# Where the dot products of the second residual gate stand: in the merge or behind the second row block, in a two-layer encoder trunk on one Trainium2 core

## The chip, the cores and the metric

The kernel runs on one core of one Trainium2 chip. The core has five engines that run side by side, each with its own queue of instructions in a fixed order: TensorE (PE in the profile, with its weight loads as PEld), VectorE (DVE), ScalarE (ACT), GpSimd (POOL) and SyncE (SP), which here only issues the transfers of the weights from the chip's memory. An instruction starts when the one before it on its engine is done and the semaphores that it waits for have been raised. The metric is device microseconds (us) of one execution of the whole program, less is better.

## The reference

A bidirectional encoder of two layers on 256 positions of 1024 channels, all in float32. Each layer adds two sub-layers to the residual x, both steered by a vector c:

```python
c_act = silu(c)
for l in range(2):
    mod = c_act @ ada_w[l] + ada_b[l]            # 6 x 1024 numbers
    sh1, sc1, g1, sh2, sc2, g2 = split(mod, 6)
    h = rmsnorm(x, norm1_g[l]) * (1 + sc1) + sh1
    x = x + g1 * token_mix(h, w_in[l], w_fourier[l], w_ret[l], w_out[l])
    h = rmsnorm(x, norm2_g[l]) * (1 + sc2) + sh2
    x = x + g2 * conv_ffn(h, ffn_up[l], conv_w[l], conv_b[l], ffn_down[l])
return rmsnorm(x, final_g)
```

`token_mix` projects h, runs a Fourier branch and a retention branch, maps each to 1024 channels, and merges them: sigmoid(a_f) * y_f + sigmoid(a_r) * y_r, followed by an output projection. `conv_ffn` projects h up to two halves of 2816 channels, convolves each over three positions, multiplies gelu(first) by the second and projects down. The gate g2 is needed only after the down-projection, at the end of the layer.

## The kernel before, in words

**Precision and weights.** Each float32 operand is split into a high part of a shorter format and the rest; a product takes three matmuls (high x high, high x low, low x high: lines 149 to 151 with activations as the standing operand, line 157 with weights). So every weight block is prepared on the core: `raw()` (line 67) loads 1 MB (128 x 2048 floats) through SP into one of four raw buffers; then for each half `split` (line 61) makes the high part on ScalarE (line 63) and the low part on VectorE (line 64). A half takes one of four `wt` buffers, or a `wb` buffer of the pool for activations, where the table `plan` says so. `nextw` hands out the blocks in the order of `plan` and prepares one block ahead. A raw buffer is free again when its last reader is done, a `wt` buffer when TensorE has used it.

**Modulation vectors.** The 6 x 1024 numbers are not computed on TensorE: `ada_dots` (line 201) loads a quarter of one vector's weights (1 MB, into the same four raw buffers) and runs two dot products of 128 x 1024 with the broadcast c on VectorE (`ada_dot`, line 191; "ISA" in the order, CUSTOM_DVE_ANT_0 in the profile). Four quarters make a vector. `ada_col` does so for shift and scale (`c_sh`, `c_sc`, by way of `sct`), `ada_gate` for a gate: its dots land in `gc`, and after the fourth quarter `rows` transposes `gc` on TensorE (line 225), copies it (line 227) and sends it through memory to all partitions (lines 229 and 230). For the second gate `rows` is put into the list `behind` and is run later, in the up-projection.

**Where the quarters stand.** Lists of quarters are made per layer: G1 and G2 (gates), SC and SH (scale and shift of the second sub-layer), NX1 (the next layer's). `pl` sorts them into places, and `side(where, n)` runs the next n of a place there. In layer 0, place `h` (after each retention head) has G1, and place `c` (the merge) has SC, SH and G2 in turn, three to each of four columns. In layer 1, place `h` has SC, and place `c` has SH and G2 in turn, two to a column. Place `d` is the down-projection.

**The merge** (list MERGE, line 28; loop at line 621) goes through four columns of 256 channels, each in four steps: the two sigmoid projections, the Fourier map and the retention map. One step takes one weight block, 48 matmuls of 256 columns in two halves. At the end of a column VectorE multiplies and adds (lines 632 and 636), the result is split into `mg`, and `side("c", ...)` runs. Then the **output projection** takes four blocks wo0 to wo3 (`in_wx_dram`): wo0 and wo1 in `wt` buffers, wo2 and wo3 in `wb` buffers; for row block m = 0 and then m = 1 (128 positions each) it multiplies `mg` by all four, adds to the residual (lines 317 and 318), and prepares the normed and modulated h of the second sub-layer, `hT2` (`norm_mod`, `modulate`).

**The FFN's up-projection** does its first NX = 3 of 22 channel blocks by row blocks (loop at line 683, result `ut`): m = 0 while `hT2` of the second row block is still in the making, then m = 1. Their transposes and convolutions (`t_gated`) are put off with `later`, to be run between the halves of the blocks j = 3, 4, 5. From j = 3 on, a block is one weight block, 48 matmuls with both row blocks as one moving operand of 256 columns, then two convolutions on ScalarE (line 664) and VectorE (lines 665 and 668), a gelu, a product (line 677) and a split. `tick` counts half blocks and runs what `later` has put off.

**Order.** The program is traced in the order in which it is written; a scheduler then orders each engine's queue by readiness, with priority to what was traced first, and gives out the buffers. `tc.issue_after(ins)` forces what is traced under it behind `ins` on the engine of `ins`.

Of the kernel before, what the change touches and what calls it, by code (L numbers as in the profile page):

```python
# [21 lines left out]
NX = 3  # L22
# [6 lines left out]
def trunk(ctx, tc, a, out):  # L29
# [19 lines left out]
    def ps():  # L49
        return pp.tile([P, 512], F32, tag="ps", name="ps")  # L50
# [47 lines left out]
        plan += [(a["down"][l][:, t * 2048 : (t + 1) * 2048], int(t >= NT - 2), 0) for t in range(NT)]  # L98
    ready = []
    state = {"at": 0}  # L100
    hold = []

    def ahead(n):
# [26 lines left out]
    behind = []  # L130

    def later(n, fn):
        waiting.append([n, fn])

    def tick():
        for z in waiting:
            z[0] -= 1
        due = [z for z in waiting if z[0] <= 0]
        waiting[:] = [z for z in waiting if z[0] > 0]
        for _, fn in due:  # L140
            fn()
# [99 lines left out]
    def rstd(ss):  # L241
        V.tensor_scalar(out=ss[:, 0:1], in0=ss[:, 0:1], scalar1=ss[:, 1:2], scalar2=EPS, op0=ALU.add, op1=ALU.add)
        r = sp.tile([P, 1], F32, tag="rs", name="rs")
        G.tensor_tensor(out=r, in0=ss[:, 0:1], in1=nhalf[:, 0:1], op=ALU.pow)
        return r
# [13 lines left out]
    def norm_t(xn, pt=None):  # L259

        pt = pt or ps()
        for b in range(4):
            T.transpose(pt[:, b * P : (b + 1) * P], xn[:, b * P : (b + 1) * P], ident)  # L263
        return pt

    def modulate(l, i, m, hf, src, h, b0=0, nb=4):

        t = tmp("hm")
        for b in range(b0, b0 + nb):
            k = hf * 4 + b  # L270
            s = slice(b * P, (b + 1) * P)
            sc, sh = scA[l][i][:, k : k + 1], shB[l][i][:, k : k + 1]
            if (b + m) % 2 == 0 or nb == 1:
                A.activation(t[:, s], src[:, s], AF.Identity, scale=sc, bias=sh)  # L274
            else:
                V.tensor_scalar(out=t[:, s], in0=src[:, s], scalar1=sc, scalar2=sh, op0=ALU.mult, op1=ALU.add)
        z = slice(b0, b0 + nb)
        return split(h[:, 0, z, tok(m)], h[:, 1, z, tok(m)], t.rearrange("p (b t) -> p b t", b=4)[:, z, :])

    def norm_mod(l, i, m, hp, ss, t0, t1):  # L280

        def mod(hf):
            made = modulate(l, i, m, hf, norm_t(xns[hf]), hp[hf])
            if i == m == 0:
                hold[:] = [2, *made]

        r = rstd(ss)
        xns = [norm_s(m, r, hf) for hf in range(2)]
        for hf, t in ((0, t0), (1, t1)):
            later(t, lambda hf=hf: mod(hf))  # L290
# [12 lines left out]
    def mm_w(pt, hp, w, cut=None):  # L303


        for b in range(2):
            for k in range(KT):
                s = slice(k * P, (k + 1) * P)
                x, t = hp[k // 4], w[b]
                mm_ws(pt[:, b * S : (b + 1) * S], t[:, 0, s], t[:, 1, s], x[:, 0, k % 4, :], x[:, 1, k % 4, :],  # L310
                      k == 0, k == KT - 1, b == cut and k == 0)
            tick()
# [50 lines left out]
    for k in range(KT):  # L363
# [12 lines left out]
        for z in range(2):  # L376
            t = wt()[:, :2048].rearrange("p (s c) -> p s c", s=2)
            nh = 2 if k == 0 else 1
            for n in range(nh):
                c = slice(n * D // nh, (n + 1) * D // nh)  # L380
# [25 lines left out]
    for l in range(L):  # L406
# [50 lines left out]
        G1 = [lambda q=q: ada_gate(l, 0, q, gc1, g1) for q in range(4)]  # L457
        G2 = [lambda q=q: ada_gate(l, 1, q, gc2, g2) for q in range(4)]
        SC = [lambda q=q: ada_col(l, 1, 1, q) for q in range(4)]
        SH = [lambda q=q: ada_col(l, 1, 0, q) for q in range(4)]  # L460
        NX1 = [lambda q=q, kind=kind: ada_col(l + 1, 0, kind, q) for kind in (1, 0) for q in range(4)] if l + 1 < L else []
        if l == 0:
            pl = dict(v=[], h=G1, c=[z[i] for i in range(4) for z in (SC, SH, G2)], d=NX1)
        else:
            pl = dict(v=G1, h=SC, c=[SH[i // 2] if i % 2 == 0 else G2[i // 2] for i in range(8)], d=NX1)

        def side(where, n):
            for _ in range(n):
                if pl[where]:
                    pl[where].pop(0)()  # L470
# [212 lines left out]
        for m in range(2):  # L683
            if m == 1:
                flush()
            for j in range(NX):
                o = ps()[:, :S]
                for k in range(KT):
                    s = slice((k % 4) * S, (k % 4 + 1) * S)
                    x, t = hp2[k // 4], wx[j][k // 4]  # L690
                    mm_xs(o, x[:, 0, k % 4, tok(m)], x[:, 1, k % 4, tok(m)], t[:, 0, s], t[:, 1, s],
                          k == 0, k == KT - 1)
                if m == 1:
                    ahead((j + 1) // 2)
                ut[m][j] = tmp("ut")[:, :S]
                A.activation(ut[m][j], o, AF.Copy)
                tick()

        def t_gated(j):
# [5 lines left out]

        for j in range(NX):
            later(2 * j + 1, lambda j=j: t_gated(j))
        while behind:
            later(2 * NX - 1, behind.pop())
        for j in range(NX, FT):  # L710
            w = nextw()
            pt = ps()
            mm_w(pt, hp2, w, 1 if j == 2 * NX - 1 else None)
            gated(pt, j)

# [140 lines left out]
```

## Time and profile before

| | us |
|---|---|
| median of three runs | 889.98 (887.55 to 890.5) |
| profiled execution, whole | 888.77 |
| its span in the trace | 886.9 |
| TensorE busy | 867.5 |
| VectorE busy | 736.7 |
| ScalarE busy | 501.8 |

The span runs from the first to the last instruction that the profiler saw; the execution's own time has 1.9 us around it. In rows of the trace, the first number is the start in us from the span's start, the second the duration, then engine, line, operation and tiles as out<-in, with xcount where equal rows are merged; square brackets give the engine's idle time before the row and what ended it. In rows of waits, the three numbers are the total in us, the number of waits and the longest. In rows of stretches, each engine has its busy time and its instruction count, then come the granted clock of TensorE (1.00 is full), the busy share of the DMA engines and the GB/s that they moved. Names of the trace leave out buffer numbers; `hT2` appears there as `hT`.

Where the parts lie in the trace: the merge of layer 0 from about 150 to 237.7, its output projection to 263, the up-projection to about 387; in layer 1 the output projection begins at 670.8 and the up-projection's blocks j >= 3 at 713.1.

### The profile page before, as it was taken

Reading aid. Unit: us, or ns where it says so; the run is one execution under the profiler, and the core shown is the slowest. Engines: PE = TensorE matmul, PEld = TensorE weight load, DVE = VectorE, ACT = ScalarE, POOL = GpSimd, SP = SyncE. Lnnn points to the kernel's source line nnn. Section 1 sums busy time; section 2 is a strip of 40 time slices with the busy share of each in tenths; the row PEclk is TensorE's granted clock in tenths of the full one; section 3 lists DMA queues with packets and bytes.
Section 4 is the critical chain, followed back from the end, with each engine's and each line's share of the span. In section 5 each row is a group of like instructions: output and inputs, shape, how many; then the busy total and the mean of one; then the engine's idle time right before and its main releaser. Section 6 shows DMA issues by size and latency. Waiting matters only on the chain.

```text
span 886.9 us, 15356 instructions
## 1 busy us (share of the span) xinstructions
PE 867.5 (98%) x6250; PEld 809.2 (91%) x6250; DVE 736.7 (83%) x1135; ACT 501.8 (57%) x736; POOL 22.1 (2%) x33
## 2 busy tenths in 40 slices
PE   7999999999899999999999999999999999999996
PEld 5889999999889999998888899999998999999885
DVE  6899998888785899999787789878887769999554
ACT  5666445544465877653574554555444768777442
POOL 1000010000000000000000000000000000000000
PEclk9999999999999999999999999999999999999999
DMA  8995665788883465579856667637887455655521
GB/s 319 357 377 208 234 224 208 256 334 311 328 311 145 144 214 198 197 261 376 345 190 222 250 224 266 219 125 284 299 328 275 144 190 197 222 200 191 190 96 48
DMA packets 33032, 210.84 MB, mean 238 GB/s; under 512 B 4001, under 2 KB 4289, under 8 KB 10178
## 3 DMA queue, kind: packets, MB, share of 16 engines
q1 hardware_dynamic: 31682, 207.16, 63.7%
q0 software_dynamic: 704, 2.11, 0.7%
q8 instruction: 49, 0.80, 0.4%
q10 hardware_dynamic: 576, 0.59, 0.2%
q14 instruction: 21, 0.17, 0.1%
HBM read 208.79 MB, written 1.06 MB: 237 GB/s over the span
## 4 chain that ended last, share of the span: by engine, by line
PE 75%; DVE 13%; DMA 5%; ACT 3%; issue 3%; POOL 1%; POOLq 0%; SPq 0%; ACTq 0%; DVEq 0%
PE ps L157 41%; PE ps L150 11%; PE ps L149 11%; PE ps L151 11%; DVE wt L64 5%; DMA raw<-in_ada_dram 3%; DVE raw L193 3%; PE ps L263 1%; ACT wt L63 1%; DMA raw<-in_ww_dram 1%; DMA raw<-in_wx_dram 1%; PE ps L481 1%; DVE qk L64 1%; ACT hm L274 1%; DVE sig L632 0%
## 5 line engine op out<-in xcount | busy, mean ns | idle before, releaser
L157 PE MATMUL ps<-hT,wt 128*128 128x256 f32 (+1 forms) x3368 | 390.6, 277 | 0.0
L157 PEld LDWEIGHTS ps<-hT,wt 128*128 128x128 f32 x3368 | 386.6, 188 | 0.4
L63 ACT ACTIVATE wt<-raw 128x1024 fp32r<-128x1024 f32 (+1 forms) x270 | 281.9, 1052 | 181.2 <-PE ps L157 72.4
L64 DVE TENSOR_TENSOR wt<-raw,wt 128x1024 fp32r<-128x1024 f32 (+1 forms) x270 | 325.4, 1214 | 56.3 <-ACT wt L63 55.3
L193 DVE CUSTOM_DVE_ANT_0 raw<-raw,c_cbc,c_adab 128x1024 f32<-128x1024 f32 x96 | 121.2, 1279 | 17.8 <-DMA raw<-in_ada_dram 17.8
L151 PE MATMUL ps<-wt,hT 128*128 128x512 f32 (+1 forms) x240 | 87.1, 363 | 0.0
L150 PE MATMUL ps<-wt,hT 128*128 128x512 f32 (+1 forms) x240 | 87.0, 363 | 0.0
L149 PE MATMUL ps<-wt,hT 128*128 128x512 f32 (+1 forms) x240 | 83.8, 366 | 2.5 <-ACT wt L63 2.3
L664 ACT ACTIVATE cv<-ps,c_cvw 128x256 f32<-128x256 f32 x88 | 49.4, 562 | 29.2 <-PE ps L157 18.6
L150 PE MATMUL ps<-wt,act 128*128 128x512 f32 (+1 forms) x162 | 59.4, 367 | 0.0
L149 PE MATMUL ps<-wt,act 128*128 128x512 f32 (+1 forms) x162 | 59.3, 366 | 0.0
L151 PE MATMUL ps<-wt,act 128*128 128x512 f32 (+1 forms) x162 | 59.2, 365 | 0.0
L149 PEld LDWEIGHTS ps<-wt,hT 128*128 128x128 f32 x240 | 45.2, 189 | 10.6 <-ACT wt L63 3.2
L151 PEld LDWEIGHTS ps<-wt,hT 128*128 128x128 f32 x240 | 45.5, 190 | 7.4
L150 PEld LDWEIGHTS ps<-wt,hT 128*128 128x128 f32 x240 | 45.5, 190 | 6.8
L665 DVE SCALAR_TENSOR_TENSOR cv<-ps,c_cvw,cv 128x255 f32<-128x255 f32 x88 | 41.1, 479 | 6.4 <-ACT cv L664 6.4
L157 PE MATMUL ps<-yf,wt 128*128 128x256 f32 x384 | 45.0, 277 | 0.0
L157 PE MATMUL ps<-yrT,wt 128*128 128x256 f32 x384 | 45.0, 277 | 0.0
L157 PEld LDWEIGHTS ps<-yrT,wt 128*128 128x128 f32 x384 | 44.3, 188 | 0.0
L157 PEld LDWEIGHTS ps<-yf,wt 128*128 128x128 f32 x384 | 44.3, 188 | 0.0
L668 DVE SCALAR_TENSOR_TENSOR cv<-ps,c_cvw,cv 128x255 f32<-128x255 f32 x88 | 41.2, 480 | 1.6
L149 PEld LDWEIGHTS ps<-wt,act 128*128 128x128 f32 x162 | 30.6, 189 | 5.1
(154 smaller groups left out, 942.0 us busy)
## 6 DMA issues: line engine op xcount, KB each, us to landing
raw<-in_ww_dram SPq DMA_DIRECT2D x48, 1024.0 KB, 5.5
raw<-in_ada_dram SPq DMA_DIRECT2D x40, 1024.0 KB, 5.9
raw<-in_up_dram SPq DMA_DIRECT2D x38, 1024.0 KB, 4.8
raw<-in_wx_dram SPq DMA_DIRECT2D x24, 1024.0 KB, 6.6
raw<-in_down_dram SPq DMA_DIRECT2D x22, 1024.0 KB, 4.9
raw<-in_ada_dram SPq DMA_DIRECT2D x16, 512.0 KB, 8.4
raw<-in_wx_dram SPq DMA_DIRECT2D x16, 512.0 KB, 7.9
raw<-in_upx_dram SPq DMA_DIRECT2D x6, 1024.0 KB, 6.6
```

The source lines that it names most:

```text
L63: h = A.activation(dst_h, src if hi_src is None else hi_src, AF.Copy)
L64: l = V.tensor_tensor(out=dst_l, in0=src, in1=dst_h.bitcast(F32), op=ALU.subtract)
L149: T.matmul(pt, xh, wh, start=start, stop=False)
L150: T.matmul(pt, xh, wl, start=False, stop=False)
L151: T.matmul(pt, xl, wh, start=False, stop=stop)
L157: T.matmul(pt[:, z], w, x[:, z], start=start and i == 0, stop=stop and i == 2)
L193: V.tensor_tensor_reduce(out=wb, in0=wb, in1=cbc, scale=1.0, scalar=adab[:, l, v * KT + k : v * KT + k + 1], op0=ALU.mult, op1=ALU.add, ac ...
L263: T.transpose(pt[:, b * P : (b + 1) * P], xn[:, b * P : (b + 1) * P], ident)
L274: A.activation(t[:, s], src[:, s], AF.Identity, scale=sc, bias=sh)
L664: A.activation(o, pt, AF.Identity, scale=cvw[:, l, 1, c : c + 1], bias=cvw[:, l, 3, c : c + 1])
L665: V.scalar_tensor_tensor(out=o[:, 1:], in0=pt[:, : S - 1], scalar=cvw[:, l, 0, c : c + 1], in1=o[:, 1:], op0=ALU.mult, op1=ALU.add)
L668: V.scalar_tensor_tensor(out=o[:, : S - 1], in0=pt[:, 1:], scalar=cvw[:, l, 2, c : c + 1], in1=o[:, : S - 1], op0=ALU.mult, op1=ALU.add)
```

## The change

The four quarters of G2 leave the merge in both layers. They get a place of their own, `u`, in the up-projection: one quarter after each of the three channel blocks of the second row block, and the last one when block j = 3 begins. The dots of the first three are forced behind the last split of `hT2` on VectorE (`last_h[1]`, noted by `mod` in `norm_mod`). The rest of the gate (`rows`, by way of `behind`) is put off at block j = 3 and runs after as many half blocks as before. In the merge, layer 0 now has two quarters to a column, layer 1 one.

```diff
@@ -98,6 +98,7 @@
         plan += [(a["down"][l][:, t * 2048 : (t + 1) * 2048], int(t >= NT - 2), 0) for t in range(NT)]
     ready = []
     state = {"at": 0}
+    last_h = []
     hold = []
 
     def ahead(n):
@@ -283,6 +284,7 @@
             made = modulate(l, i, m, hf, norm_t(xns[hf]), hp[hf])
             if i == m == 0:
                 hold[:] = [2, *made]
+            last_h[:] = made
 
         r = rstd(ss)
         xns = [norm_s(m, r, hf) for hf in range(2)]
@@ -460,9 +462,9 @@
         SH = [lambda q=q: ada_col(l, 1, 0, q) for q in range(4)]
         NX1 = [lambda q=q, kind=kind: ada_col(l + 1, 0, kind, q) for kind in (1, 0) for q in range(4)] if l + 1 < L else []
         if l == 0:
-            pl = dict(v=[], h=G1, c=[z[i] for i in range(4) for z in (SC, SH, G2)], d=NX1)
+            pl = dict(v=[], h=G1, c=[z[i] for i in range(4) for z in (SC, SH)], u=G2, d=NX1)
         else:
-            pl = dict(v=G1, h=SC, c=[SH[i // 2] if i % 2 == 0 else G2[i // 2] for i in range(8)], d=NX1)
+            pl = dict(v=G1, h=SC, c=SH, u=G2, d=NX1)
 
         def side(where, n):
             for _ in range(n):
@@ -694,6 +696,9 @@
                     ahead((j + 1) // 2)
                 ut[m][j] = tmp("ut")[:, :S]
                 A.activation(ut[m][j], o, AF.Copy)
+                if m == 1:
+                    with tc.issue_after(last_h[1]):
+                        side("u", 1)
                 tick()
 
         def t_gated(j):
@@ -705,11 +710,12 @@
 
         for j in range(NX):
             later(2 * j + 1, lambda j=j: t_gated(j))
-        while behind:
-            later(2 * NX - 1, behind.pop())
         for j in range(NX, FT):
             w = nextw()
             pt = ps()
+            if j == NX:
+                side("u", 1)
+                later(2 * NX - 1, behind.pop())
             mm_w(pt, hp2, w, 1 if j == 2 * NX - 1 else None)
             gated(pt, j)
```

How this moves VectorE's queue at the end of layer 0's merge. The names: `raw_2625` and `raw_2630` hold the last quarters of scale and shift, `raw_2634` the last of G2; `wt_2566` and `wt_2569` are the halves of wo0 (`raw_2564`), `wt_2640` and `wt_2643` of wo1 (`raw_2638`); L632 and L636 are the merge's products and sum in `sig`. Before, from the product of the last column's third step on:

```order
L632 TENSOR_TENSOR sig_2444<-ps_2505,sig_2444 128x512
L64 TENSOR_TENSOR wt_2569<-raw_2564,wt_2569 128x1024
L193 ISA raw_2630,c_sh01_98<-raw_2630,c_cbc_73,c_adab_78 128x1024
L193 ISA c_sh01_98 128x1
L193 ISA raw_2634,gc_599<-raw_2634,c_cbc_73,c_adab_78 128x1024
L193 ISA gc_599 128x1
L193 ISA raw_2634,gc_599<-raw_2634,c_cbc_73,c_adab_78 128x1024
L193 ISA gc_599 128x1
L632 TENSOR_TENSOR sig_2503<-ps_2563,sig_2503 128x512
L64 TENSOR_TENSOR wt_2640<-raw_2638,wt_2640 128x1024
L636 TENSOR_TENSOR sig_2444<-sig_2444,sig_2503 128x512
L64 TENSOR_TENSOR wt_2643<-raw_2638,wt_2643 128x1024
```

In the change (the numbers of buffers and lines differ: `wt_2557` is the second half of wo0, `wt_2624` and `wt_2627` are wo1, `wb_2632` and `wb_2635` wo2):

```order
L634 TENSOR_TENSOR sig_2432<-ps_2493,sig_2432 128x512
L64 TENSOR_TENSOR wt_2557<-raw_2552,wt_2557 128x1024
L64 TENSOR_TENSOR wb_2632<-raw_2630,wb_2632 128x1024
L64 TENSOR_TENSOR wt_2624<-raw_2622,wt_2624 128x1024
L634 TENSOR_TENSOR sig_2491<-ps_2551,sig_2491 128x512
L64 TENSOR_TENSOR wb_2635<-raw_2630,wb_2635 128x1024
L638 TENSOR_TENSOR sig_2432<-sig_2432,sig_2491 128x512
L64 TENSOR_TENSOR wt_2627<-raw_2622,wt_2627 128x1024
L64 TENSOR_TENSOR mg_1543<-sig_2432,mg_1543 128x512
```

The dots of the last shift quarter (`raw_2618`) now stand ahead of wo0's first half, those of the gate are gone, and between the product and wo1's first half are two splits in place of four dots, a split and a product. wo2's first half has moved ahead of wo1's, its second half ahead of wo1's second.

VectorE's queue behind the last split of `hT2` in layer 0. Before (`wt_3013` to `wt_3136` are halves of the up-projection's blocks j = 3, 4 and 5, `cv_3086` is the first convolution):

```order
L64 TENSOR_TENSOR hT2_2663<-hm_2925,hT2_2663 128x4x128
L64 TENSOR_TENSOR wt_3013<-raw_3011,wt_3013 128x1024
L64 TENSOR_TENSOR wt_3016<-raw_3011,wt_3016 128x1024
L64 TENSOR_TENSOR wt_3050<-raw_3048,wt_3050 128x1024
L64 TENSOR_TENSOR wt_3053<-raw_3048,wt_3053 128x1024
L64 TENSOR_TENSOR wt_3136<-raw_3134,wt_3136 128x1024
L665 SCALAR_TENSOR_TENSOR cv_3086<-ps_3081,c_cvw_595,cv_3086 128x255
L668 SCALAR_TENSOR_TENSOR cv_3086<-ps_3081,c_cvw_595,cv_3086 128x255
```

In the change (`raw_2970`, `raw_3009` and `raw_3040` hold the first three quarters of G2, `wt_3001` and `wt_3004` block j = 3):

```order
L64 TENSOR_TENSOR hT2_2647<-hm_2909,hT2_2647 128x4x128
L194 ISA raw_2970,gc_599<-raw_2970,c_cbc_73,c_adab_78 128x1024
L194 ISA gc_599 128x1
L194 ISA raw_2970,gc_599<-raw_2970,c_cbc_73,c_adab_78 128x1024
L194 ISA gc_599 128x1
L64 TENSOR_TENSOR wt_3001<-raw_2999,wt_3001 128x1024
L64 TENSOR_TENSOR wt_3004<-raw_2999,wt_3004 128x1024
L194 ISA raw_3009,gc_599<-raw_3009,c_cbc_73,c_adab_78 128x1024
L194 ISA gc_599 128x1
L194 ISA raw_3009,gc_599<-raw_3009,c_cbc_73,c_adab_78 128x1024
L194 ISA gc_599 128x1
L194 ISA raw_3040,gc_599<-raw_3040,c_cbc_73,c_adab_78 128x1024
```

Two dots now stand ahead of block j = 3's halves and four between them and those of j = 4; behind j = 4's follow the two dots of the fourth quarter (`raw_3053`), and only then the first convolution. The halves of j = 5, one of which stood ahead of the first convolution, now stand inside it. SP's queue has the four loads there too: the first ahead of block j = 3's, two between j = 3's and j = 4's, and the last behind j = 4's.

A little later on VectorE, at the convolution of block j = 3 (`cv_3122`). Before (`wt_3317` is the first half of block j = 7; `wt_3225`, the second half of j = 6, stands further ahead):

```order
L668 SCALAR_TENSOR_TENSOR cv_3126<-ps_3056,c_cvw_595,cv_3126 128x255
L668 SCALAR_TENSOR_TENSOR cv_3172<-ps_3167,c_cvw_595,cv_3172 128x255
L677 TENSOR_TENSOR cv_3122<-cv_3122,cv_3126 128x256
L64 TENSOR_TENSOR wt_3317<-raw_3315,wt_3317 128x1024
L64 TENSOR_TENSOR act_2840<-cv_3122,act_2840 128x256
```

In the change:

```order
L670 SCALAR_TENSOR_TENSOR cv_3126<-ps_3052,c_cvw_595,cv_3126 128x255
L670 SCALAR_TENSOR_TENSOR cv_3172<-ps_3167,c_cvw_595,cv_3172 128x255
L679 TENSOR_TENSOR cv_3122<-cv_3122,cv_3126 128x256
L64 TENSOR_TENSOR wt_3225<-raw_3220,wt_3225 128x1024
L64 TENSOR_TENSOR act_2824<-cv_3122,act_2824 128x256
```

At the same convolution the queue now splits the second half of j = 6, and the first half of j = 7 comes one convolution later; so it goes on until block j = 9. In layer 1 the three places look alike. TensorE's own order is the same in both kernels.

## The prediction

> **What bounds the kernel now.** I read the busy totals first, then the waits of TensorE, then the stretches around the change.
>
> ```profile
> PE 867.5 (98%) x6250; PEld 809.2 (91%) x6250; DVE 736.7 (83%) x1135; ACT 501.8 (57%) x736; POOL 22.1 (2%) x33
> ...
> PE ps L149 <- ACT wt L63: 3.9, 2, 2.3
> PE ps L150 <- DVE wt L64: 2.3, 2, 1.3
> PE ps L263 <- DVE xn L254: 2.3, 2, 1.9
> PE ps L181 <- DMA c_cbc<-in_crow_dram: 2.3, 1, 2.3
> ```
>
> TensorE is busy for 867.5 us of a span of 886.9, and the change leaves its instructions and their order as they are. So the end can only move by what TensorE waits, 19.4 us in all, and most of that (the start, the retention heads, the border of the layers) lies far from the change. Where the change works there are two places, both where the merge hands over to the output projection. In layer 0, TensorE's rows in order of time:
>
> ```profile
> 237.74 0.40 PE L149 MATMUL ps<-wt,mg 128*128 128x512 f32 x1
> ...
> 240.26 0.39 PE L151 MATMUL ps<-wt,mg 128*128 128x512 f32 x1
> 242.26 0.49 PE L149 MATMUL ps<-wt,mg 128*128 128x512 f32 x1 [1.61 <-ACT wt L63]
> 244.06 0.50 PE L150 MATMUL ps<-wt,mg 128*128 128x512 f32 x1 [1.31 <-DVE wt L64]
> 244.40 0.40 PE L151 MATMUL ps<-wt,mg 128*128 128x512 f32 x1
> ...
> 245.32 0.39 PE L149 MATMUL ps<-wt,mg 128*128 128x512 f32 x1
> 245.80 0.50 PE L150 MATMUL ps<-wt,mg 128*128 128x512 f32 x1
> 246.14 0.39 PE L151 MATMUL ps<-wt,mg 128*128 128x512 f32 x1
> ```
>
> Starts lie 0.23 us apart when nothing is awaited (245.32 is four matmuls behind 244.40). Over that, the five long steps lose 1.77 + 1.57 + 0.11 + 0.25 + 0.11 = **3.81 us**. The projection has done the 12 matmuls of its first weight block (wo0) and waits for the second (wo1). In layer 1:
>
> ```profile
> 675.06 0.39 PE L149 MATMUL ps<-wt,mg 128*128 128x512 f32 x1
> 676.48 0.50 PE L150 MATMUL ps<-wt,mg 128*128 128x512 f32 x1 [1.03 <-DVE wt L64]
> 676.82 0.39 PE L151 MATMUL ps<-wt,mg 128*128 128x512 f32 x1
> ```
>
> 1.19 + 0.11 = **1.30 us**, again in wo1.
>
> Why wo1 is late: the transfers, SP's row, ScalarE's row and the chain of waits.
>
> ```profile
> 222.08 8.66 DMA raw<-in_ada_dram
> ...
> 234.53 0.63 SPq L70 DMA_DIRECT2D raw<-in_wx_dram  x1
> ...
> 241.15 2.00 ACT L63 ACTIVATE wt<-raw 128x1024 fp32r<-128x1024 f32 x2 [7.59 <-DMA raw<-in_wx_dram]
> ```
>
> wo1's load is issued at 234.53 and is there just before 241.15, 6.6 us later. It could not be issued sooner, because its raw buffer (one of four) held the last scale quarter, whose load took from 222.08 to 230.74 and whose second dot ended at 234.5. Each merge column of layer 0 passes four weight blocks and three ada quarters through those four buffers.
>
> **The change part by part.** *Removed from the merge*, in each layer: four ada loads of 1 MB and eight dots.
>
> ```profile
> L193 DVE DVE_READ_ACCUMULATOR2_ANT gc<- x8: 80/84/86, 174.6 to 242.2; 128x1 f32 x8
> ...
> 239.77 1.28 DVE L193 CUSTOM_DVE_ANT_0 raw<-raw,c_cbc,c_adab 128x1024 f32<-128x1024 f32 x1
> 240.98 0.09 DVE L193 DVE_READ_ACCUMULATOR2_ANT gc<- 128x1 f32 x1
> 240.98 1.28 DVE L193 CUSTOM_DVE_ANT_0 raw<-raw,c_cbc,c_adab 128x1024 f32<-128x1024 f32 x1
> 242.19 0.08 DVE L193 DVE_READ_ACCUMULATOR2_ANT gc<- 128x1 f32 x1
> 242.19 0.69 DVE L632 TENSOR_TENSOR sig<-ps,sig 128x512 f32<-128x512 f32 x1
> ```
>
> A dot takes the queue 1.21 us (239.77 to 240.98 to 242.19; reading the accumulator hides in the next start), so eight take 9.7 us. TensorE pays none of it as such: it pays because the dots hold a raw buffer and stand ahead of the split of wo1 (242.79).
>
> *What wo1 meets in the change, layer 0*, on before's clock. The raw buffer still comes from the last scale quarter. Its load can now start when step 1 of the last column is split. That split waits for weight buffers that TensorE leaves at 215.98 (the row below), then 1.05 us of ScalarE and 1.2 of VectorE: 218.3. With 5 to 6.6 us for a load and the dots behind the next splits, those end near 226, wo1 is issued then and lands by 233, 8 us before it does now. What is late next is its weight buffer, not its data: the second half goes where the last merge step's second half lies, which TensorE leaves at 237.74. ScalarE's 1.05 us and the short VectorE queue behind it (one sig product, one split, one add: 0.6 + 1.13 + 0.6) put wo1's second split at 240.3 to 241.5; TensorE wants it at 237.74 + 18 x 0.227 + 0.23 = 242.05. So about 0.5 us of air: the wait goes, and at worst (the split one instruction later) 0.7 us of it stays. wo2 and wo3 are wanted from 243.2 and have their own buffers.
>
> ```profile
> 215.98 6.28 PE L157 MATMUL ps<-hT,wt 128*128 128x256 f32 x54
> ```
>
> *Layer 1.* There VectorE stands 2.23 us before the wo2 split that is queued ahead of wo1's, because wo2's load came late:
>
> ```profile
> 670.59 1.23 DVE L64 TENSOR_TENSOR wb<-raw,wb 128x1024 fp32r<-128x1024 f32 x1 [2.23 <-ACT wb L63]
> ...
> 675.20 1.22 DVE L64 TENSOR_TENSOR wt<-raw,wt 128x1024 fp32r<-128x1024 f32 x1
> ...
> 663.11 6.37 DMA raw<-in_wx_dram
> ```
>
> With one ada quarter to a column instead of two, wo2 takes the buffer of the last shift quarter near 659 and not at 663.11, lands near 664 to 666, and the 2.23 us close; wo1's second split then ends near 673.7, for a matmul at 675.29. The 1.30 us go. Nothing behind the handover needs the earlier TensorE to be met by anything but VectorE's usual work: the residual and norm chain hangs on TensorE's own outputs and shifts with them.
>
> *Added: the head of the FFN.* The eight dots come right behind the last split of hT2 on VectorE (all of them ahead of the first convolution). The stretches:
>
> ```profile
> core 0: us, PE busy (x) PEld busy (x) DVE busy (x) ACT busy (x) POOL busy (x), PEclk, DMA share, GB/s
> ...
> 237.70:252.70 15.00, 11.99 (x51) 8.86 (x51) 14.49 (x18) 6.99 (x8) 0.00 (x0) 1.00 0.99 372
> ...
> 275.10:297.10 22.00, 22.00 (x191) 22.00 (x191) 12.99 (x17) 13.83 (x20) 0.00 (x0) 1.00 0.39 138
> 297.10:335.00 37.90, 37.90 (x337) 37.88 (x336) 37.08 (x72) 28.61 (x53) 1.13 (x2) 1.00 0.58 203
> ```
>
> From 275.1 to 297.1 VectorE is busy 12.99 of 22.00 us: 9.0 us are free, for 9.7 us of dots. That is the cover. Its largest piece:
>
> ```profile
> 274.48 0.69 DVE L64 TENSOR_TENSOR hT<-hm,hT 128x512 fp32r<-128x512 f32 x1 [0.32 <-ACT hT L63]
> ...
> 286.69 1.23 DVE L64 TENSOR_TENSOR wt<-raw,wt 128x1024 fp32r<-128x1024 f32 x1 [4.16 <-ACT wt L63]
> ```
>
> In the new order: two dots to 277.5, two splits to 279.8, four dots to 284.6, two splits to 286.9 (TensorE wants them from 288.7), two dots to 289.3, then the first convolution, which now begins at 287.83. The two splits at 284.6 need their load, issued when the first dots free a buffer at 277.5 and 4.8 us under way:
>
> ```profile
> raw<-in_up_dram SPq DMA_DIRECT2D x4, 1024.0 KB, 4.8
> ```
>
> 282.3, plus 1.05 us of ScalarE: in time. The last gate load starts at 279.8 and lands before 286.9. Behind that the remaining gaps before the convolutions (0.5 to 0.7 us each, waits for ScalarE) are filled, and VectorE is 0.2 to 0.6 us late at 297. I take **0 us** for TensorE, with 0.6 us late as the input of the next step.
>
> *The stretch after it has no free time* (37.08 of 37.90), so lateness and order count. Weight splits and convolutions alternate:
>
> ```profile
> 309.12 1.23 DVE L64 TENSOR_TENSOR wt<-raw,wt 128x1024 fp32r<-128x1024 f32 x1
> ...
> 312.49 1.23 DVE L64 TENSOR_TENSOR wt<-raw,wt 128x1024 fp32r<-128x1024 f32 x1
> ...
> 297.87 24.40 PE L157 MATMUL ps<-hT,wt 128*128 128x256 f32 x213
> ```
>
> One split per 3.37 us against 24 matmuls in 2.72 (213 in 24.13 us): the lead melts by 0.65 a step until the backlog of convolutions is gone. The split at 312.49, done at 313.7, is the closest: TensorE begins with it seven steps after 297.87, near 317.0 (297.87 + 7 x 2.72), a lead of 3.3 us. In the change one more convolution (4 x 0.39 + 0.33 + 0.34 = 2.23 us) stands ahead of each of these splits; with 0.2 to 0.6 us late the closest lead is **0.5 to 0.9 us**. Below it TensorE feels nothing; each us beyond it costs a us, once in each layer. The bound from above, if none of the 9.0 us took a dot: 9.7 + 2.23 - 3.3 = 8.6 us a layer; from below nothing can be won, since TensorE waits for nothing from 275 to 345.
>
> *Sum:* 3.81 + 1.30 = 5.1 us. The profiled execution took 888.77 us (span 886.9 and 1.9 around it); less 5.1 is 883.7. It lies 1.2 below the median of the three runs (889.98), which would give 884.9. I say **884.5**.
>
> **The rivals.** *Late by order, no change (chance 0.2).* The lead of 0.5 to 0.9 us rests on ScalarE keeping up: in the new order two weight splits stand on it between the two halves of the first convolution, and the second half waits for a buffer that TensorE frees at 288.5. If each such step costs 1 to 1.5 us more, VectorE is 3 us late, the lead of 3.3 - 2.23 = 1.1 is gone, and TensorE stands about 2 us in each layer: 5.1 - 4 = 1.1 won, 888.5. For it: all gaps of VectorE there end on ScalarE. Against it: ScalarE is busy 13.83 of 22.00 us there.
>
> *Slower (0.12).* The free time at the head is not usable: the 4.16 us gap returns, because the loads of the next weight blocks are now issued only after dots have freed their buffers, and SP takes them in order. Then VectorE is 4.2 + 0.6 us late, TensorE stands 4.8 - 1.1 = 3.7 us in each layer, and 7.4 - 5.1 = 2.3 us is lost: 892. It decides from 3.7 us late at 297 (1.1 to use up the lead, 2.6 to use up half the gain). For it: four more loads in the same buffers. Against it: the DMA engines are 0.39 busy there, and the needed loads have 2 us to spare in the count above.
>
> How long a wait stays its own price is a question of the clock: the row of 237.70 to 252.70 holds waits of 1.61 and 1.31 us, and its granted clock is 1.00. By the Trainium skill ("TensorE: Matmul & The Clock Gate", Part 1) an idle window of about 3.4 us halves the clock until 3.4 us of work have passed. By that rule, and as an estimate from its figures, a wait of 3.7 us in one piece could cost up to 1.7 us more, and this rival would end near 895; by the trace's clock it stays at 892. No stretch of the FFN shown here waits long enough to tell, and the sum above holds no such wait.
>
> *Only part of the waits goes (0.1).* wo1's second split stays behind its buffer in layer 0 (0.7 us) and wo2's load still comes late in layer 1 (1.3 us): 3.1 won, 886.5.
>
> **How the numbers follow.** Forecast (both waits go, nothing comes back, 4 to 5.2 us won): 0.58. About 0.3% (2.7 us) is what a measurement of this kernel tells from no change. Forecast and part count as faster: 0.68; late by order as same: 0.2; slower 0.12. The range runs from the full 5.1 us and the lowest run shown (887.55 - 5.1 = 882.4) to the case of no change, 889.5; beyond it lies the slower rival.
>
> **What would show it.** In the changed profile TensorE has no wait over 0.3 us at the handover, in either layer; wo1's load is issued more than 8 us ahead of the last merge step's end; VectorE has no gap of 4 us behind hT2; TensorE waits for no split between 275 and 345 on before's clock. It is wrong if TensorE waits for `wt` of line 64's helper about 35 to 45 us after hT2 (the lead was too short), at the first up-projection block (a load or dots too late), or still at wo1.

## The result, and the profile after

| us | before | the change |
|---|---|---|
| median, seven runs of each | 889.98 (885.99 to 892.92) | 883.82 (882.68 to 886.32) |
| profiled execution, its span | 888.77, 886.9 | 883.82, 882.0 |

The ratio is 0.9946, with a 95% interval of 0.9922 to 0.9971: 4.8 us less, between 2.6 and 6.9 (6.2 by the medians). Two later comparisons with the same kernel gave 884.68 against 889.53 and 884.52 against 889.88. Line numbers of the changed kernel are one to six above those of before: 150 to 152 are the matmuls that were 149 to 151, 194 is the dot, 264 the transposes of the norm.

The busy totals of the changed kernel's page:

```profile
PE 866.7 (98%) x6250; PEld 809.9 (92%) x6250; DVE 736.6 (84%) x1135; ACT 500.5 (57%) x736; POOL 22.1 (3%) x33
```

and TensorE's waits, all of them:

```profile
PE ps L264 <- DVE xn L255: 2.5, 2, 2.1
PE ps L150 <- ACT wt L63: 2.3, 1, 2.3
PE ps L182 <- DMA c_cbc<-in_crow_dram: 2.3, 1, 2.3
PE ps L158 <- ACT qk L63: 0.4, 1, 0.4
PE ps L150 <- ACT hT L63: 0.2, 1, 0.2
PE ps L158 <- DVE qk L64: 0.2, 1, 0.2
```

TensorE and VectorE do the same work as before (866.7 and 736.6 us busy, the same counts). The waits for weights at the handovers, `ACT wt` and `DVE wt` with 1.6 + 2.3 us before, are gone; the 2.3 us for `ACT wt` that is left is the first weight block of the kernel. By the starts of TensorE's rows the two handovers lose nothing any more, where before they lost 5.1 us; the span is 4.9 us shorter.

At the handover of layer 0, SP's, ScalarE's, VectorE's and TensorE's rows:

```profile
228.20 5.77 SPq L70 DMA_DIRECT2D raw<-in_wx_dram  x3
...
236.25 1.06 ACT L63 ACTIVATE wb<-raw 128x1024 fp32r<-128x1024 f32 x1 [1.35 <-DMA raw<-in_wx_dram]
...
241.96 1.22 DVE L64 TENSOR_TENSOR wt<-raw,wt 128x1024 fp32r<-128x1024 f32 x1
...
239.07 0.40 PE L150 MATMUL ps<-wt,mg 128*128 128x512 f32 x1
...
243.18 0.40 PE L150 MATMUL ps<-wt,mg 128*128 128x512 f32 x1
243.41 0.40 PE L151 MATMUL ps<-wt,mg 128*128 128x512 f32 x1
243.65 0.40 PE L152 MATMUL ps<-wt,mg 128*128 128x512 f32 x1
```

wo1's load is issued 10.9 us ahead of the projection's first matmul (239.07), where it was 3.2 us ahead before. The projection runs through wo1 without a bracket. But wo1's second split ends at 243.18, and the matmul that needs it (line 151) starts at 243.41: 0.23 us of air. And ScalarE stands 1.35 us for the load of wo2 (`wb`), whose split its queue has ahead of wo1's; that comes back below. In layer 1, VectorE's second split of wo1 and the matmul that needs it:

```profile
670.43 1.22 DVE L64 TENSOR_TENSOR wt<-raw,wt 128x1024 fp32r<-128x1024 f32 x1
...
672.09 0.39 PE L151 MATMUL ps<-wt,mg 128*128 128x512 f32 x1
```

No wait either, with 0.4 us of air (671.65 to 672.09).

The stretches behind `hT2`, which before had 12.99 of 22.00 and 37.08 of 37.90 us of VectorE busy, in the changed kernel:

```profile
272.00:294.00 22.00, 22.00 (x195) 22.00 (x195) 21.96 (x35) 13.64 (x21) 0.00 (x0) 1.00 0.82 314
294.00:332.00 38.00, 38.00 (x337) 37.98 (x337) 37.11 (x70) 27.50 (x50) 1.13 (x2) 1.00 0.57 200
```

The closest weight split in them, and TensorE's rows above it:

```profile
312.50 1.22 DVE L64 TENSOR_TENSOR wt<-raw,wt 128x1024 fp32r<-128x1024 f32 x1
...
294.74 35.50 PE L158 MATMUL ps<-hT,wt 128*128 128x256 f32 x311
```

The 9 us of free time are filled but for 0.04 us, and TensorE is busy without a gap. The split of block j = 9's first half ends at 313.72. Seven half blocks lie ahead of that block in the row that starts at 294.74: 170 matmuls, two more than 7 x 24, because two of them run in two pieces. Their starts put the block's first matmul at 314.09 and its third, the first to need this split, at 314.32. The lead is 0.6 us.

### The profile page after: what moved, and what is told of

It is laid out like the page before. It is cut to its first block, busy times and chain, and to the rows that moved or that the text cites. A ratio compares the mean times of both kernels' runs of the same rounds, so it can differ in the third digit from the quotient of the medians.

```text
span 882.0 us, 15355 instructions
## 1 busy us (share of the span) xinstructions
PE 866.7 (98%) x6250; PEld 809.9 (92%) x6250; DVE 736.6 (84%) x1135; ACT 500.5 (57%) x736; POOL 22.1 (3%) x33
## 4 chain that ended last, share of the span: by engine, by line
PE 87%; DVE 8%; ACT 2%; issue 2%; POOL 1%; DMA 0%; POOLq 0%; SPq 0%; ACTq 0%
PE ps L158 52%; PE ps L150 11%; PE ps L152 11%; PE ps L151 11%; DVE wt L64 2%; DVE raw L194 1%; PE ps L264 1%; PE ps L483 1%; DVE qk L64 1%; ACT hm L275 1%; DVE rc L521 0%; DVE rsn L522 0%; ACT wt L63 0%; PE ps L615 0%; DMA c_xs<-in_xs_dram 0%
```

## The experiments

Each run is set beside runs of before on the same chip; "excess" is what TensorE's starts lose against its normal pitch at a place, summed over the first row block of the output projection where a handover is meant. The changed kernel has 0.0 in both handovers.

**One layer at a time.** `pl` of one layer is put back:

```diff
 e1_layer0:
-            pl = dict(v=G1, h=SC, c=SH, u=G2, d=NX1)
+            pl = dict(v=G1, h=SC, c=[SH[i // 2] if i % 2 == 0 else G2[i // 2] for i in range(8)], u=[], d=NX1)
 e2_layer1:
-            pl = dict(v=[], h=G1, c=[z[i] for i in range(4) for z in (SC, SH)], u=G2, d=NX1)
+            pl = dict(v=[], h=G1, c=[z[i] for i in range(4) for z in (SC, SH, G2)], u=[], d=NX1)
```

> Layer 0 as in the change, layer 1 as before. Theory (each layer's handover is a wait of its own): TensorE's waits at layer 0's handover are gone (3.81 us less), those of layer 1 stay at about 1.30 us; time 3.8 us below before, about 886.2 if before is at 890. Rival (the gain is one thing, such as less traffic overall): layer 1's wait shrinks too, or layer 0's doesn't go.

> Layer 1 as in the change, layer 0 as before. Theory: layer 0's handover keeps 3.8 us of waits, layer 1's 1.30 us are gone; time 1.3 us below before, inside what can be measured. Rival: as for the run with layer 0 alone.

Layer 0 alone: 885.08 against 889.56, ratio 0.9954 (0.9938 to 0.9969), 4.5 us less by the medians; excess 0.3 at layer 0's handover, 1.05 at layer 1's. Layer 1 alone: 887.57 against 889.56, ratio 0.9978 (0.9965 to 0.9991), 2.0 us less; excess 4.3 and 0.0. The two parts are independent and, within their intervals, add up to the whole. Of the 4.3 us in the second run, 1.6 are no wait: matmuls at half the clock behind it (last section).

**Which part of the move, the loads or the dots?** One kernel puts G2's loads back into the merge with a tiny reader, one puts dots back without loads; in both the gate itself is computed as in the change. (The scratch tile `junkd` and the `return w` of `ada_dots` are left out here.)

```diff
 def ada_col(l, i, kind, q):
     if kind == 0:
 e3_loads, behind ada_dots:
+        if i == 1:
+            w = raw(a["ada"][l, 5, q])
+            V.tensor_tensor(out=junkd[:, 0:2], in0=w[:, 0:2], in1=w[:, 1024:1026], op=ALU.add)
 e4_dots:
-        ada_dots(l, 3 * i, q, shB[l][i])
+        w = ada_dots(l, 3 * i, q, shB[l][i])
+        if i == 1:
+            for b in range(2):
+                ada_dot(l, 5, 2 * q + b, w[:, b * D : (b + 1) * D], junkd)
```

> The change, and in each merge the four 1 MB loads of G2 are made as before into the raw buffers, read there by one sum of two columns instead of two dots (the gate itself is computed in the up-projection as in the change). Theory (the buffer is what makes wo1 late): wo1's load in layer 0 is issued late again and TensorE waits 1.5 to 3.5 us at that handover, of 3.81 before. Rival (VectorE's time is what makes it late): under 0.5 us. Layer 1: 0 to 1.3 us by the theory.

> The change, and in each merge every shift quarter's dots are run a second time on the same buffer into a scratch tile: the eight dots of before without their four loads. Theory (buffer): wo1's data is there in time and TensorE waits 0 to 0.5 us at layer 0's handover, since wo1's second split comes at about the same place and had 0.2 us of air. Rival (VectorE's time): 2.4 us more of VectorE less 0.2 of air, so 2.2 us or more, up to the 3.81 of before.

With the loads alone, TensorE's rows at layer 0's handover and SP's issue of wo1 to wo3:

```profile
234.35 5.68 SPq L70 DMA_DIRECT2D raw<-in_wx_dram  x3
...
242.61 0.49 PE L150 MATMUL ps<-wt,mg 128*128 128x512 f32 x1 [2.19 <-ACT wt L63]
243.87 0.50 PE L151 MATMUL ps<-wt,mg 128*128 128x512 f32 x1 [0.77 <-DVE wt L64]
...
245.38 0.63 PE L150 MATMUL ps<-wt,mg 128*128 128x512 f32 x1
245.81 0.63 PE L151 MATMUL ps<-wt,mg 128*128 128x512 f32 x1
```

wo1 is issued at 234.35, as in before (234.53), and the wait is back: 2.35 + 1.03 = 3.4 us of excess, of 3.81. With the dots alone, SP's, ScalarE's and TensorE's rows:

```profile
228.90 7.95 SPq L70 DMA_DIRECT2D raw<-in_wx_dram  x3
...
237.40 1.06 ACT L63 ACTIVATE wb<-raw 128x1024 fp32r<-128x1024 f32 x1 [3.45 <-DMA raw<-in_wx_dram]
...
244.20 0.50 PE L151 MATMUL ps<-wt,mg 128*128 128x512 f32 x1 [1.57 <-DVE wt L64]
```

wo1 is issued early (228.90) and lands in time, and yet 1.74 us come back; the bracket now names VectorE. So the loads are the larger cause in layer 0, as the prediction had it, but "0 to 0.5 us" for the dots was wrong. The dots act in two ways, which this run does not separate. They take VectorE 2.4 us a column, with 0.23 us of air. They also stand ahead of splits whose raw buffers the next loads need: the last scale quarter is issued 17.2 us ahead of the projection's start instead of 19.0, wo2 lands 0.75 us ahead of it instead of 2.85, and ScalarE stands 3.45 us for wo2, where it stood 1.35. In layer 1 either one alone brings the wait back (1.2 us by the loads, 1.6 by the dots, of 1.30). Each of the two kernels was timed once; the rows, not the times, carry this.

**Where the dots go.** Three other places for the four pairs, and two more pairs on top (the lines that keep `last_w` and `junkd` are left out):

```diff
 e6_5678 (e7_tail: (11, 13, 15, 17), and 17 in place of 8); the call behind the second row block is left out
-            if j == NX:
+            if j in (5, 6, 7, 8):
                 side("u", 1)
-                later(2 * NX - 1, behind.pop())
+            if j == 8:
+                later(3, behind.pop())
 e8_free
                 if m == 1:
-                    with tc.issue_after(last_h[1]):
-                        side("u", 1)
+                    side("u", 1)
 e5_two, at j == NX, behind side("u", 1)
+                for b in range(4):
+                    ada_dot(l, 5, b, last_w[0][:, (b % 2) * D : (b % 2 + 1) * D], junkd)
```

> The change, and behind the fourth quarter's dots two more pairs of dots on the same buffer into a scratch tile, in each layer: 4.8 us more of VectorE at the head, no more loads. Theory (the head's free time is used up by the change, and 0.6 to 0.9 us of lead is what is left at block j = 9): TensorE waits 2.2 to 3.3 us in each layer, near the first half of j = 9 or of j = 5 or later where the order in between changes; 4.4 to 6.6 us in all, so 888 to 891 against 884 for the change. Rival (the head has room still): no wait, 884.

> Out of the merge as in the change, but the four quarters stand at blocks j = 5, 6, 7 and 8, without being forced behind hT2. Theory (it is the free time behind hT2 that takes the dots; later VectorE has none): the 4.2 us gap takes one pair, 7.2 us come on top of a lead of 3.3 to 3.8, and TensorE waits 1.6 to 4.7 us in each layer around j = 9 or 10, so 887 to 893. Rival (to be out of the merge is all that counts): 884 as the change, no waits between hT2 and the down-projection.

> Out of the merge, the four quarters at blocks j = 11, 13, 15 and 17, behind the place of the shortest lead. Theory: the leads there are 4 to 5 us and VectorE has 3.7 us free up to the end of the up-projection, so 9.7 us of dots nearly fit: TensorE waits 0 to 2 us in each layer, late in the up-projection, 884 to 888. Rival: leads there don't hold because the weight buffers are what limits the splits, 4 us or more in each layer, 892.

> The change without the dots being forced behind the last split of hT2. The first pair then stands on VectorE ahead of the norm of a row block, and TensorE's own order shifts (four matmuls of the up-projection's first block come ahead). Theory: 1.2 to 2.4 us of dots stand in the chain residual, norm, hT2, of which TensorE feels what its other work doesn't cover: 0 to 2.4 us in each layer, 884 to 889. Rival (the forced place is no matter): 884, no new wait in the rows around hT2.

| run | median us | against before (95%) | new excess of TensorE, layer 0 and 1 |
|---|---|---|---|
| two more pairs | 890.09 | 1.0011 (0.9991 to 1.0031) | waits of 1.8 and 1.9, at j = 5, 9 and 10; 3.3 at layer 0's handover (below) |
| at j = 5 to 8 | 893.51 | 1.0063 (1.0043 to 1.0083) | waits of 2.9 and 2.5, at j = 9 and 10 |
| at j = 11 to 17 | 886.71 | 0.9976 (0.9962 to 0.9990) | none in the up-projection, 0.6 in layer 0's down-projection |
| not forced behind `hT2` | 891.57 | 1.0041 (1.0027 to 1.0056) | waits of 3.2 and 4.6 in the norm chains |

Two more pairs are felt, at j = 9 among others, where the lead was shortest: the room behind `hT2` is used up. (The waits are somewhat under the 2.2 us expected; the cause of that is open.) At j = 5 to 8, where VectorE has no free time, the same four pairs turn the gain into a loss of 0.6%. So being out of the merge is not enough. In that run's profile the waits, 5.4 us, are only a part of the loss: behind the second one 1.6 us go to half the clock and 2.6 us to a slower pitch (both in the last section). Late in the up-projection the dots fit without a wait there, and still the time lies 2 us above the change's. TensorE's rows show 0.6 of it in the down-projection, 0.6 in layer 1's handover, and in this profile 1.5 us of the slower pitch, from 365 to 385 and from 796 to 821. So a place behind the shortest lead keeps a part of the gain too; the 9 us behind `hT2` are the best of the places tried. And without the forced place the waits were above the 2.4 us a layer that was expected at most. VectorE's rows in that run show why:

```profile
266.83 1.27 DVE L194 CUSTOM_DVE_ANT_0 raw<-raw,c_cbc,c_adab 128x1024 f32<-128x1024 f32 x1
...
268.03 0.20 DVE L243 TENSOR_SCALAR ss<-ss 128x1 f32<-128x1 f32 x1
268.16 1.27 DVE L194 CUSTOM_DVE_ANT_0 raw<-raw,c_cbc,c_adab 128x1024 f32<-128x1024 f32 x1
...
269.88 0.49 DVE L255 TENSOR_SCALAR xn<-c_xs,rs 128x512 f32<-128x512 f32 x1 [0.44 <-POOL rs L245]
270.28 1.28 DVE L194 CUSTOM_DVE_ANT_0 raw<-raw,c_cbc,c_adab 128x1024 f32<-128x1024 f32 x1
...
271.49 0.73 DVE L277 TENSOR_SCALAR hm<-ps,c_sc,c_sh 128x128 f32<-128x128 f32 x2
272.13 1.28 DVE L194 CUSTOM_DVE_ANT_0 raw<-raw,c_cbc,c_adab 128x1024 f32<-128x1024 f32 x1
```

I had counted one pair in the chain. Six of the eight dots in layer 0 and seven in layer 1 stand ahead of the last split of `hT2`, between the steps of the norm: the sum of squares (`ss`) and `hm` come directly behind a dot, while `xn` still waits for GpSimd.

**What is left at the handover.** In the profile of the run with two more pairs, layer 0's handover had 2.9 us of waits, though its order there is that of the change. Two runs were to tell whether wo2's load is the cause: the change again, and the change with the splits of wo2 and wo3 forced behind wo1's on both engines.

```diff
 e9_order (wo_at holds the place of wo1 in plan; its making and that of wo1 are left out)
-                    split(t[:, 0, :], t[:, 1, :], w[:, c * 1024 : (c + 1) * 1024])
+                    at = state["at"] - 1
+                    for ins in wo1 if at - 1 in wo_at or at - 2 in wo_at else ():
+                        order.enter_context(tc.issue_after(ins))
+                    made = split(t[:, 0, :], t[:, 1, :], w[:, c * 1024 : (c + 1) * 1024])
+                    if at in wo_at:
+                        wo1[:] = made
```

> The change, and at both handovers the splits of wo2 and wo3 forced behind those of wo1 on ScalarE and VectorE; no other engine's order moves. Theory (what is left at the handover is wo2's late load standing ahead of wo1's splits, in some executions only): wo1's second split ends about 1.2 us earlier (1.4 instead of 0.2 us of air), no wait of TensorE there whatever wo2's load takes, and the median lies 0 to 1.5 us below the change measured beside it, with fewer executions 2 to 3 us above the lowest. Rival (the spread of the change comes from elsewhere, such as the clock at the start): the same median and the same spread. If wo2 or wo3 now come too late: 0.5 us or more of waits on wb in the output projections, and slower.

> The change itself once more, to have its median beside the run with the moved splits: about 884, 5 us below before; in its trace the handover of layer 0 has either no wait (wo2's load under 6 us) or 1 to 3 us of waits (wo2's load near 7 us).

> The splits of wo2 and wo3 behind wo1's, once more, to set its median beside the change's with twice the executions. Theory (wo2's late load costs the change something in some executions): again 0.5 to 2 us below the change beside it. Rival (the spread is TensorE's pitch of 117.7 in place of 113.3 ns in long stretches, which falls on either kernel): within 0.5 us of it, and a stretch of 117.7 ns in the traces of slower executions of either.

> The change beside it, 883.5 to 885. If its trace has no wait at the handover again, four of its profiles or those with its order there (the change, the second run of it, layer 0 alone, the quarters at j = 5 to 8) have none, and only one has.

The third profile of the change (885.84 us, where the second took 882.03) has the wait. ScalarE's, VectorE's and TensorE's rows:

```profile
238.98 1.06 ACT L63 ACTIVATE wb<-raw 128x1024 fp32r<-128x1024 f32 x1 [4.52 <-DMA raw<-in_wx_dram]
239.95 1.04 ACT L63 ACTIVATE wt<-raw 128x1024 fp32r<-128x1024 f32 x1
...
240.08 1.22 DVE L64 TENSOR_TENSOR wb<-raw,wb 128x1024 fp32r<-128x1024 f32 x1 [2.60 <-ACT wb L63]
241.22 1.22 DVE L64 TENSOR_TENSOR wt<-raw,wt 128x1024 fp32r<-128x1024 f32 x1
...
242.49 0.50 PE L151 MATMUL ps<-wt,mg 128*128 128x512 f32 x1 [0.72 <-DVE wt L64]
...
245.96 0.50 PE L151 MATMUL ps<-wt,mg 128*128 128x512 f32 x1 [1.58 <-DVE wt L64]
```

wo1's load had landed at 234.85, and ScalarE stood 4.52 us in front of wo2, whose load took 6.74 us in this execution and 5.0 in the two others of the change. The excess of that handover is 3.13 us here, 0.03 and 0.12 there: one program, two outcomes. Of the eight profiles whose queues at layer 0's handover are those of the change, six have 0.3 us or less of excess there, and two have 3.1 and 3.3.

wo2's long load is only half of it, and the cause begins one load earlier. VectorE's first dot of the last scale quarter, in the profile of 885.84 us and in that of the changed kernel above (883.82 us):

```profile
227.35 1.28 DVE L194 CUSTOM_DVE_ANT_0 raw<-raw,c_cbc,c_adab 128x1024 f32<-128x1024 f32 x1 [2.04 <-DMA raw<-in_ada_dram]
```

```profile
225.68 1.28 DVE L194 CUSTOM_DVE_ANT_0 raw<-raw,c_cbc,c_adab 128x1024 f32<-128x1024 f32 x1
```

In all eight profiles that quarter's load is issued 19.0 us ahead of the projection. In the six it is there when VectorE comes to it; in the two VectorE stands 2.0 us for it, since it takes 7.5 and 7.6 us. wo1 waits for this quarter's buffer, and wo2 is issued 6.4 us ahead of the projection instead of 7.8. Then wo2 also takes 6.7 and 7.0 us instead of 4.9 to 5.3, and lands 0.3 and 0.5 us behind the projection's start. What makes the quarter's load slow in these two is open.

| us | change | wo2 behind wo1 | before |
|---|---|---|---|
| first comparison, six runs each | 884.68 (882.03 to 886.38) | 882.96 (881.62 to 885.89) | 889.53 |
| second comparison, six runs each | 884.52 (882.28 to 885.84) | 882.83 (882.29 to 885.45) | 889.88 |

With the splits moved, the medians lie 1.7 us lower both times, at 0.9934 (0.9915 to 0.9952) and 0.9927 (0.9903 to 0.9951) of before, and eight of twelve runs are below 883.1 us, where four of all nineteen of the change are. Both of its profiles have no excess at either handover, but in both the last scale quarter was in time, and the change's own order has next to none then. So no trace shows the new order with a late load; its worth rests on the times. ScalarE's, VectorE's and TensorE's rows of the second:

```profile
235.33 1.06 ACT L63 ACTIVATE wt<-raw 128x1024 fp32r<-128x1024 f32 x1 [1.65 <-PE ps L166]
...
239.38 1.22 DVE L64 TENSOR_TENSOR wt<-raw,wt 128x1024 fp32r<-128x1024 f32 x1
...
237.85 0.40 PE L158 MATMUL ps<-wt,mg 128*128 128x512 f32 x1
```

ScalarE now waits for TensorE to leave wo1's first buffer, 2.5 us ahead of the projection, where in the profile of 885.84 us it came to that split 1.3 us behind the projection's start (239.95 against 238.64). wo1's second split ends at 240.6, and its matmul comes 4.34 us behind 237.85, at 242.2: 1.6 us of air, 1.4 expected. The intervals overlap those of the change (0.9938 to 0.9969 and 0.9911 to 0.9958), and the means of the twelve runs lie 1.1 us apart, so 1 to 2 us is likely and not certain. Its own runs still reach 885.9: the profile of 885.40 us has a cause of another kind, told in the last section.

## Why the prediction was right, step by step

- **The bound.** TensorE's work and order stayed the same, and the forecast gain came where it was forecast: 5.1 us of excess at the handovers, and 884.5 forecast against medians of 883.8, 884.7 and 884.5. That the span is 4.9 us shorter, so near to 5.1, is partly luck. Set beside before matmul by matmul, the changed profile loses 1.5 us in its first 20 us (its matmuls go at a step of 0.43 us until 20.1, those of before until 17.0), and it gains 1.1 us away from the handovers, most of it where before has the slower pitch of the last section. The two layers' shares, 3.81 and 1.30, were 4.5 and 2.0 by the times of the single-layer runs, each within its interval.
- **Why wo1 was late.** The loads alone bring 3.4 of 3.8 us back in layer 0. The prediction named the raw buffer that they hold. That they also slow each other down was not tested apart from it: the last scale quarter's load took 8.7 us in before (222.08 to 230.74) and 8.4 with the loads alone, and at most 5.6 in the changed kernel. In layer 1 the prediction named wo2's late load only; there the dots without loads bring the whole wait back, by which of their two ways is open. wo1 was forecast to be issued near 226 and there by 233 on before's clock; with the projection starting 1.3 us later in the changed execution (239.07 against 237.74), it was issued at 226.9 and landed at 232.3.
- **The air at the handover** was mis-sized. Forecast was 0.5 us in layer 0 and, in layer 1, a split done 1.6 us early; measured were 0.23 and 0.4. The step that failed is the sentence that wo2 and wo3 "have their own buffers": they do, but their splits stand ahead of wo1's in ScalarE's and VectorE's queues, and wo2's load comes last. In the changed kernel's profile above it cost nothing; in the execution of 885.84 us it cost 3.1. The rival "only part of the waits goes" was not the typical case, but it does happen, and through this door.
- **The free time behind `hT2`.** 9.0 us for 9.7 of dots: VectorE is busy 21.96 of 22.00 us there, TensorE feels nothing, and the closest lead, forecast at 0.5 to 0.9 us, is 0.6. That this fits is partly luck. The lead before was 3.7 us and not 3.3 (the third matmul of the block, which needs the split, starts at 317.46 there, and the split ends at 313.72), and the change took 3.1 of it, where 2.4 to 2.8 had been counted. Two more pairs cost 1.8 us of waits a layer, and the same pairs behind the free time 2.5 to 2.9, so this place is the cover, and it is used up.
- **The rivals.** Late by order, and the slower case, did not come: the needed loads were there, and no gap of VectorE opened. The runs at j = 5 to 8 and without the forced place show that the slower side was real: 0.4 to 0.6% slower than before with the same dots in another place.
- **The clock.** The prediction counted each wait at its own price, and in the profile of before it was so. It isn't so in general: in two profiles that have layer 0's wait (layer 1 alone, and the loads alone) the clock fell behind waits of 1.2 + 0.8 and 2.2 + 0.8 us. That before's executions pay this now and then would make the gain larger than 5.1; no run here counts how often.

## What to carry to other kernels

Work that nothing waits for is free only where its engine has idle time, or where the work behind it has a lead. So look for such a stretch by windows and place the work there by force; left to readiness it can slip into the next dependent chain. When a wait goes, read what is next in the same queue: a split whose data comes last, standing ahead of one whose data is there, can be a wait that some executions have and others don't, and one profile doesn't show it. Follow such a wait back past the load that it names to what held up its issue. Take several profiles of the same program before trusting an air of 0.2 us.

## What the runs showed of the hardware

**Half the clock behind short waits.** In the run with the loads alone, the rows at 245.38 and 245.81 above lie 0.43 us apart, where 0.23 is normal. The stretch in the windows:

```profile
242.00:244.00 2.00, 0.62 (x2) 0.32 (x3) 1.41 (x2) 1.51 (x2) 0.00 (x0) 1.00 0.81 303
244.00:246.00 2.00, 2.00 (x7) 1.45 (x8) 2.00 (x3) 0.94 (x2) 0.00 (x0) 0.71 0.97 381
246.00:248.00 2.00, 2.00 (x7) 1.45 (x5) 1.37 (x3) 1.70 (x2) 0.00 (x0) 0.50 0.98 414
248.00:250.00 2.00, 2.00 (x10) 1.63 (x9) 1.86 (x3) 1.82 (x2) 0.00 (x0) 0.94 1.04 438
```

The granted clock is 0.50 for some 3.4 us, 1.6 us lost. Before's waits of 1.61 and 1.31 us, and single waits of 2.30 and 1.98 us in the unforced run, were not followed by it. One of 1.94 us in layer 1 of that same run was, and one of 2.00 us at layer 1's j = 9, in the run at j = 5 to 8. The length of the wait alone doesn't decide.

What decides can be read from the 14 traces. In each, all changes of the granted clock lie whole multiples of 3.41 us apart. Cut into stretches of 3.41 us on that grid, the unforced run has these around its waits of 2.30 and 1.94 us:

```profile
688.65:692.06 3.41, 1.50 (x11) 1.44 (x12) 2.97 (x5) 2.14 (x4) 1.24 (x1) 1.00 0.43 123
702.30:705.72 3.42, 1.48 (x14) 1.28 (x13) 2.98 (x6) 1.26 (x3) 1.53 (x1) 1.00 0.93 355
705.72:709.13 3.41, 3.41 (x18) 3.41 (x18) 3.18 (x7) 2.13 (x6) 0.00 (x0) 0.50 0.74 259
```

With 1.50 us of TensorE busy the clock stays; with 1.48 it halves for the next stretch. From the first change of the clock on, every stretch of the 14 traces with 1.48 us or less of TensorE busy is followed by half the clock, and none with 1.50 or more is. Below the limit are the four behind the waits named so far (1.42 to 1.48), the ends of the programs, and five stretches at the start, behind the wait for the first weight block. In before's handover the two stretches with the waits have 1.82 and 2.08. So a wait of about 2 us costs 1.6 us more or nothing, by how it lies on the grid. The busy time is the profile's, with modelled ends of matmuls, so the limit is known only as this profile counts it. The Trainium skill ("TensorE: Matmul & The Clock Gate", Part 1) speaks of an activity window of about 3.4 us that runs freely. The traces agree with the 3.4 us and the free run, and not with the reading that a wait has to fill a window of 3.4 us.

**Two pitches at full clock.** Matmuls of 128x256 followed each other in 113.3 ns in most stretches and in 117.7 in some, at a granted clock of 1.00 in both. The same stretch of layer 1's merge, first in the 885.40 us profile with wo2 behind wo1, then in the 882.03 us profile of the change:

```profile
620.00:640.00 20.00, 20.00 (x172) 20.00 (x172) 13.01 (x15) 9.04 (x10) 0.00 (x0) 1.00 0.63 218
```

```profile
620.00:640.00 20.00, 20.00 (x178) 20.00 (x178) 13.49 (x15) 10.02 (x11) 0.00 (x0) 1.00 0.71 252
```

172 against 178 matmuls in 20 us. The slower pitch held from 607 to 668, which costs 2.3 us and is about what sets that execution above the others of its kernel. In the run with two more pairs it began right behind a wait of 0.36 us (at 324.08) and held for 66 us, to the end of layer 0's up-projection: a wait that costs 0.4 us by itself was followed by 2.5 more. Every one of the 14 traces has such stretches, several at much the same places (580 to 601 in before, 577 to 598 in the changed kernel); how long they hold differs. What decides between the two pitches is open; the runs here were not made for it.
